# An early 64-byte write into every 256 KB of the output, in an embedding gather with position add

## The chip, the cores and the metric

One core of one Trainium2 chip. The metric is the device time of one execution in microseconds (us), the median of several runs. Times are compared only with those of the kernel before on the same occasion, on the same chip. For what lies inside a trace, traces of different occasions are compared as well.

## The reference

```
indices [32, 512] int32 below 50000; embedding_table [50000, 512] f32; position_embed [512, 512] f32
out[b, s, :] = embedding_table[indices[b, s], :] + position_embed[s, :]        # [32, 512, 512] f32
```

16,384 rows of 2,048 B are gathered from random places of a table of 102.4 MB, and 33.55 MB are written. Nothing is computed but one add per element.

## The kernel before

A sequence's 512 rows lie as 4 rows on each of 128 partitions. GpSimd (POOL) issues 128 gathers of 128 rows, VectorE (DVE) adds the position block in place, and SyncE (SP) stores two gathers at a time (one at a time for the first four and the last four). There are 23 slots of 1 MB, so that no gather waits for a slot before the 24th sequence.

```python
        load_pos(nc.sync, 1)
        # ... (all indices)
        nc.sync.wait_ge(s_pos[half - 1], 16)
        load_pos(nc.sync, half)
        nc.sync.wait_ge(s_gather[0], 16)
        load_pos(nc.sync, half + 1)

        nc.gpsimd.memset(ones[:], 1.0).then_inc(s_ident, 1)
        # ...
        for g, (b, k) in enumerate(order):
            # ... (waits for the index tiles; for a slot from the 24th sequence on)
            ins = nc.gpsimd.indirect_dma_start(
                out=slots[b % SLOTS][:, k, :], out_offset=None, in_=table,
                in_offset=bass.IndirectOffsetOnAxis(ap=where, axis=0),
            ).then_inc(s_gather[g % LANES], 16)
        # ...
            nc.vector.tensor_tensor(
                out=part, in0=part, in1=pos_ps[:, k, :], op=add
            )._wait_ge(s_gather[g % LANES], rounds(g)).then_inc(s_add, 1)
        # ...
        rest = 0
        for adds, b, at, n in stores:
            done = s_out.get(b, s_rest)
            rest += done is s_rest
            nc.sync.dma_start(
                out=out_rows[b][:, at : at + n, :],
                in_=slots[b % SLOTS][:, at : at + n, :],
            )._wait_ge(s_add, adds).then_inc(done, 16)
        nc.sync.wait_ge(s_rest, 16 * rest)
```

## Time and profile before

| | before |
|---|---|
| time, median of 3 runs | 183.71 us (183.7 to 183.91) |
| the execution whose trace is read | 176.13 us, of which the span is 174.4 |
| POOL busy, DVE busy | 121.9 us, 89.0 us |
| DMA | 68.34 MB, 392 GB/s on average |
| last byte of the last store leaves at | 172.50 us of the span |

The traced execution is 7.6 us shorter than the timed ones.

Part 3 and part 6 of the profile page of the kernel before: the DMA queues (packets, MB, share of 16 engines' time), and the issues (count, KB each, median us from issue to landing).

```profile
q1 hardware_dynamic: 11056, 34.76, 49.6%
q0 software_dynamic: 10240, 33.56, 48.9%
...
out_dram<-slot SPq DMA_DIRECT2D x60, 512.0 KB, 6.5
...
slot<-in_embedding_table_dram,idx_t POOLq DMA_INDIRECT x112, 7.3
pos_sb<-in_position_embed_dram SPq DMA_DIRECT2D x4, 256.0 KB, 3.9
...
idx<-in_indices_dram SPq DMA_DIRECT2D x1, 4.0 KB, 1.6
```

Gathers (q0) and plain transfers (q1) share the 16 DMA engines half and half, and together take 98.5% of their time.

### The profile page before, as it was taken

Reading aid. Unit: us, or ns where it says so; the run is one execution under the profiler, and the core shown is the slowest. Engines: PE = TensorE matmul, PEld = TensorE weight load, DVE = VectorE, ACT = ScalarE, POOL = GpSimd, SP = SyncE. Lnnn points to the kernel's source line nnn. Section 1 sums busy time; section 2 is a strip of 40 time slices with the busy share of each in tenths; the row PEclk is TensorE's granted clock in tenths of the full one; section 3 lists DMA queues with packets and bytes.
Section 4 is the critical chain, followed back from the end, with each engine's and each line's share of the span. In section 5 each row is a group of like instructions: output and inputs, shape, how many; then the busy total and the mean of one; then the engine's idle time right before and its main releaser. Section 6 shows DMA issues by size and latency. Waiting matters only on the chain.

```text
span 174.4 us, 427 instructions
## 1 busy us (share of the span) xinstructions
PE 1.0 (1%) x4; PEld 0.4 (0%) x4; DVE 89.0 (51%) x133; ACT 3.6 (2%) x5; POOL 121.9 (70%) x134
## 2 busy tenths in 40 slices
PE   0001100000000000000000000000000000000000
PEld 0000000000000000000000000000000000000000
DVE  0316744745555546455655555555555555555550
ACT  2210000000000000000000000000000000000000
POOL 4777777777777777777777777777777777777200
DMA  3889999999999999999999999999999999999994
GB/s 100 251 260 399 364 385 398 398 396 413 417 418 415 416 420 420 419 420 418 419 420 417 419 421 418 420 419 419 419 418 420 419 419 420 420 417 420 418 413 169
DMA packets 21299, 68.34 MB, mean 392 GB/s; under 512 B 3760, under 2 KB 3888, under 8 KB 21296
## 3 DMA queue, kind: packets, MB, share of 16 engines
q1 hardware_dynamic: 11056, 34.76, 49.6%
q0 software_dynamic: 10240, 33.56, 48.9%
q14 instruction: 3, 0.02, 0.0%
HBM read 34.75 MB, written 33.55 MB: 392 GB/s over the span
## 4 chain that ended last, share of the span: by engine, by line
POOL 65%; issue 22%; DMA 8%; DVE 1%; POOLq 1%; SPq 0%
POOL slot L141 65%; DMA slot<-in_embedding_table_dram,idx_t 4%; DMA slot<-in_embedding_table_dram,idx 3%; DMA idx<-in_indices_dram 1%; DVE idx_t L170 1%; POOLq L149 1%; DVE slot L176 0%; POOLq L136 0%; SPq L221 0%; POOLq L133 0%; SPq L102 0%
## 5 line engine op out<-in xcount | busy, mean ns | idle before, releaser
L141 POOL DMA_INDIRECT slot<-in_embedding_table_dram,idx_t x112 | 105.9, 945 | 34.1 <-issue 34.1
L176 DVE TENSOR_TENSOR slot<-slot,pos_ps 128x512 f32<-128x512 f32 x128 | 87.8, 687 | 80.8 <-DMA slot<-in_embedding_table_dram,idx_t 63.0
L141 POOL DMA_INDIRECT slot<-in_embedding_table_dram,idx x16 | 15.3, 958 | 5.9 <-issue 4.3
L182 ACT COPY pos_ps<-pos_sb 128x512 f32<-128x512 f32 x4 | 2.4, 589 | 8.8 <-DMA pos_sb<-in_position_embed_dram 8.8
L182 ACT ACT_TABLE_LOAD x1 | 1.3, 1283 | 1.0 <-SPq L102 1.0
L170 DVE CAST idx_t<-turned 32x128 int32<-32x128 f32 x4 | 1.1, 280 | 0.1
L154 PE MATMUL turned<-ident,idx_f 128*32 128x128 f32 x4 | 1.0, 416 | 16.9 <-DVE idx_f L164 16.9
L122 POOL MEMSET ones<- 128x128 f32 x1 | 0.2, 204 | 0.5 <-SPq L102 0.5
L154 PEld LDWEIGHTS turned<-ident,idx_f 128*32 128x32 f32 x4 | 0.4, 134 | 17.0 <-DVE idx_f L164 16.9
L123 POOL TENSOR_SCALAR_AFFINE_SELECT ident<-ones 128x128 f32<-128x128 f32 x1 | 0.3, 287 | 0.1
L210 POOL MEMSET const-float32-0.0<- 128x1 f32 x1 | 0.1, 98 | 0.3 <-issue 0.3
L164 DVE CAST idx_f<-idx_raw 128x128 f32<-128x128 int32 x1 | 0.2, 220 | 0.0
L210 POOL MEMSET const-uint8-127<- 128x1 uint8 x1 | 0.1, 115 | 0.0
L210 POOL MEMSET const-bfloat16-1.0<- 128x1 bf16 x1 | 0.1, 109 | 0.0
L210 POOL MEMSET const-float32-1.0<- 128x1 f32 x1 | 0.1, 101 | 0.0
## 6 DMA issues: line engine op xcount, KB each, us to landing
out_dram<-slot SPq DMA_DIRECT2D x60, 512.0 KB, 6.5
out_dram<-slot SPq DMA_DIRECT2D x8, 256.0 KB, 4.8
slot<-in_embedding_table_dram,idx_t POOLq DMA_INDIRECT x112, 7.3
pos_sb<-in_position_embed_dram SPq DMA_DIRECT2D x4, 256.0 KB, 3.9
slot<-in_embedding_table_dram,idx POOLq DMA_INDIRECT x16, 6.0
idx_raw<-in_indices_dram SPq DMA_DIRECT2D x1, 128.0 KB, 3.2
idx<-in_indices_dram SPq DMA_DIRECT2D x1, 4.0 KB, 1.6
idx<-in_indices_dram SPq DMA_DIRECT2D x1, 12.0 KB, 2.6
```

Of the source, the lines that this page charges most:

```text
L122: nc.gpsimd.memset(ones[:], 1.0).then_inc(s_ident, 1)
L123: nc.gpsimd.affine_select(out=ident[:], in_=ones[:], pattern=[[-1, P]], compare_op=mybir.AluOpType.is_equal, fill=0.0, base=0, channel_mul ...
L141: ins = nc.gpsimd.indirect_dma_start(out=slots[b % SLOTS][:, k, :], out_offset=None, in_=table, in_offset=bass.IndirectOffsetOnAxis(ap=whe ...
L149: nc.gpsimd.drain()
L154: ins = nc.tensor.transpose(turned[:, k].rearrange("p b j -> p (b j)"), idx_f[:, :, k], ident[:])
L164: nc.vector.tensor_copy(out=idx_f[:].rearrange("r p k -> r (p k)"), in_=idx_raw[:, :, 0])._wait_ge(s_raw, 16).then_inc(s_cast, 1)
L170: nc.vector.tensor_copy(out=idx_t[j * Q : (j + 1) * Q, :, :], in_=turned[:, :, :, j]).then_inc(s_idx, 1)
L176: nc.vector.tensor_tensor(out=part, in0=part, in1=pos_ps[:, k, :], op=add)._wait_ge(s_gather[g % LANES], rounds(g)).then_inc(s_add, 1)
L182: nc.scalar.copy(out=pos_ps[:, k, :], in_=pos_sb[:, k, :])._wait_ge(s_pos[k], 16).then_inc(s_ps, 1)
L210: nc = _bacc.Bacc("TRN2", target_bir_lowering=False, num_devices=1)
```

## The change

The intent: if the first write to a part of the output is slow, pay for it while the DMA engines have little to do, so that the stores don't. One DMA on the scalar engine's queue, before anything else there, writes 64 B at the start of each of 128 pieces of 256 KB. The stores overwrite these bytes; the sync engine waits for the touch before its first store.

```diff
+    s_touch = sem("s_touch")
...
+        nc.scalar.dma_start(
+            out=out.rearrange("b (c r) d -> (b c) r d", c=P // B)[:, 0, 0:16],
+            in_=ones[:, 0:16],
+        )._wait_ge(s_ident, 1).then_inc(s_touch, 16)
...
+        nc.sync.wait_ge(s_touch, 16)
         rest = 0
         for adds, b, at, n in stores:
```

## The prediction

> **What bounds the kernel now.** I read the page first (engine shares, slices, DMA issues), then the chain that ended last, then the waits, then a table of windows, and last the single DMA packets that the trace records.
>
> The chain of the whole span, and the waits of the engine that starts the gathers:
>
> ```profile
> POOL 65%; issue 22%; DMA 8%; DVE 1%; POOLq 1%; SPq 0%
> ...
> POOL slot L141 <- issue: 38.4, 126, 0.3
> POOL slot L141 <- DMA idx<-in_indices_dram: 1.3, 1, 1.3
> ...
> POOL slot L141 <- DVE idx_t L170: 0.3, 1, 0.3
> ```
>
> The reader is to see that the chain lies on POOL, which writes one gather's descriptors after another (0.95 us busy, 0.30 us to the next), and that POOL hardly ever waits for data: one 1.3 us wait for the first indices, one of 0.3 us at the hand-over to the second index tile. The last gathers are at the same pace:
>
> ```profile
> 160.61 0.94 POOL L141 DMA_INDIRECT slot<-in_embedding_table_dram,idx_t  x1 [0.30 <-issue]
> 161.60 0.69 DVE L176 TENSOR_TENSOR slot<-slot,pos_ps 128x512 f32<-128x512 f32 x1 [0.76 <-DMA slot<-in_embedding_table_dram,idx_t]
> 161.86 0.95 POOL L141 DMA_INDIRECT slot<-in_embedding_table_dram,idx_t  x1 [0.30 <-issue]
> ```
>
> The second gather starts at 4.34 us and the 128th at 161.86: (161.86 - 4.34) / 126 = 1.250 us each. One gather brings 128 x 2,048 B = 262,144 B and its sum is stored once, so this pace asks 524,288 B / 1.25 us = 419 GB/s of the DMA engines. The slices and the windows show that they give just that, and no more:
>
> ```profile
> DMA  3889999999999999999999999999999999999994
> GB/s 100 251 260 399 364 385 398 398 396 413 417 418 415 416 420 420 419 420 418 419 420 417 419 421 418 420 419 419 419 418 420 419 419 420 420 417 420 418 413 169
> ...
> 6.00:8.00 2.00, 0.00 (x0) 0.00 (x0) 0.71 (x2) 0.38 (x1) 1.48 (x2) 1.00 0.82 246
> 8.00:10.00 2.00, 0.00 (x0) 0.00 (x0) 0.67 (x1) 0.00 (x0) 1.61 (x2) 1.00 0.74 154
> 10.00:12.00 2.00, 0.00 (x0) 0.00 (x0) 0.36 (x1) 0.59 (x1) 1.39 (x3) 1.00 0.88 253
> ...
> 60.00:100.00 40.00, 0.00 (x0) 0.00 (x0) 21.99 (x32) 0.00 (x0) 30.25 (x33) 1.00 1.03 419
> ```
>
> In the window lines the last two columns are the busy share of the DMA engines and GB/s. From 60 us on the engines are full at 419 GB/s. From 6 to 12 us they are 74 to 88% busy but move only 154 to 253 GB/s: packets are slow there. Gathers issued into that stretch leave a backlog: the first gather landed 3.8 us after its issue, the typical later one 7.3 us (DMA issues of the page), and the last still 7.32 us. Supply and capacity are equal, so a backlog of about 7.3 - 3.8 = 3.5 us is never worked off, and **the span ends when the DMA engines have emptied it**. Two limits therefore sit within 3.5 us of each other: POOL's pace, and the DMA engines' work plus what they lost early.
>
> So the change is worth what it gives back of DMA time lost before about 60 us, and at most about 3.5 us of 183.71 (1.9%), since below that POOL's pace holds the end.
>
> **What the Trainium skill says.** "DMA: Bandwidth & Descriptors", section Specifications, gives 512 B as the least size at line rate and says that below it the engine does a read-modify-write: the 64 B touches are of that kind; no trace here shows such a write yet. The same page, section "Where 436 GB/s comes from", puts the fabric's ceiling at 435 GB/s; the trace agrees in size, 419 to 421 GB/s being the most a full slice holds. The same page, section "Issuing engines are not separate DMA queues", says that DMAs from the scalar, sync and gpsimd engines end on the same 16 engines and interleave; the trace agrees in that gathers (49%) and plain transfers (50%) share 16 engines' time. Its section "Anatomy of one DMA" puts most of the fixed cost of about 2 us on the receipt from the target memory; the smallest load of the trace (4 KB) took 1.6 us from issue to landing. I found no page that says a first access to a part of HBM is slow, on which the intent of the change rests.
>
> **The change part by part.** It removes nothing. It adds one DMA of 128 rows of 64 B (8,192 B), one row at the start of each of 128 pieces of 256 KB of the output, a wait on it ahead of the first store, and a semaphore.
>
> - *Issue on ScalarE.* It waits for the memset of the ones, which ends at 1.02 + 0.20 = 1.22 us; a DMA issue on the sync engine's sequencer takes 0.33 to 0.49 us, so I expect about 0.4 us, to 1.65. Then the activation table load (1.28 us, at 0.97 before) moves to about 1.7 and ends near 3.0. The first copy waits for the first position block until 4.35. Off the path: 0.
> - *The wait ahead of the stores.* Small loads landed 1.6 to 3.2 us after issue, so the touch should land between 3 and 4.5 us, allowing up to 6 if its packets are slow. The first store goes at 7.47 us, after its add. Slack of 3 us, and the sync engine was blocked on two earlier waits anyway (until 5.79 and about 6.75). Cost: 0.
> - *DMA time.* 8 small packets per engine. Shortest packets in the records take 7 to 9 ns; at ten to twenty times that for a read-modify-write to HBM, 8 x 0.1 to 0.2 = 0.8 to 1.6 us per engine, in 3 to 5 us, where the engines are 66 to 89% busy. The first-gather indices land at 2.61, before it. Delay of the position loads and the first gathers: 0 to 0.5 us, and part of it lies beside idle time. I book +0.1 us.
> - *The gain meant.* If the first write to a piece of the output is slow, the stores' packets should show it. I compared every packet with the usual duration of its size (159 ns for 4,096 B, 84 ns for 2,048 B) and summed the excess over 16 engines. Gathers: 1.27 us before 12 us and 1.51 after, falling off until 60 us and zero after 70. Plain queue after 12 us: 0.03 us, although 33.51 of the 33.55 MB of output leave after 12 us, always into pieces not written before. From 70 us on, 22.1 MB of stores go out without one noticeably slow packet. Before 12 us that queue lost 0.40 us between 7.4 and 12, but there it was still carrying the last position loads: the 512 packets of 2,048 B of those lie ahead of the stores in it, and 488 such packets had started by 11 us. So **the slow stretch comes before the stores' first bytes**, and belongs to the gathers from the random table rows and the position loads, which the touch doesn't reach. Gain: at most some 0.2 us.
>
> Sum: +0.1 (up to +0.5) of added DMA work, -0.1 (up to -0.2) of store packets saved: 183.71 + 0 to 0.1, so 183.8 us.
>
> **The rivals.** *The first write to a region costs, and the touch pays it in idle time.* For it: the first store, issued at 7.47 us, took 6.5 us to land, against 2.9 for the last, and the bad stretch of 6 to 12 us starts around its issue; a slow write could hold up gathers behind it without showing in its own record. Against it: the gathers' slow packets fade with time while untouched output is reached at an even rate to the end. If it holds for the first stores only, some 1 to 2 us of backlog go: 181.7 to 182.7; the ceiling is 180.2.
>
> *The touch itself is slow, and the stores wait for it.* If each of an engine's 8 writes took as long as the slowest gather packets (1.9 us), the touch would need 15 us, the first store would slip from 7.5 to some 17 us, and early gathers would suffer beside it. For it: single packets of 0.4 to 0.8 us already occur at 2.5 to 5 us. Against it: they are a minority, and stores to new pieces are at normal speed. The lost early DMA time, some 1 to 4 us, would go straight to the end: 185 to 188.
>
> *The touch delays the ninth gather.* That gather's add precedes the second index tile, and POOL took it up with 0.3 us or less of slack (20.4 us). A late ninth gather would stall POOL. But the backlog of 3.5 us keeps the DMA engines fed, so a slip of under 3 us changes nothing at the end.
>
> **Range and chances.** Timed runs scatter by 0.2 us. The range takes in a lucky saving of 1.1 us and a loss of 1.4 us: 182.6 to 185.2. Faster by over 2% needs under 180.04, below the ceiling of the gain: 0.03. Slower by over 2% needs over 187.4, the second rival at its worst: 0.03. Within 2%: 0.94.
>
> **What would show it.** Right: POOL still issues every 1.25 us; the touch lands before 6 us; the first store still goes near 7.5 us; the stretch of 6 to 12 us still moves some 150 to 250 GB/s; late gathers still take 7.2 to 7.4 us from issue to landing. Wrong towards faster: that stretch near 400 GB/s and late gathers under 6 us. Wrong towards slower: a wait of the sync engine on the touch, a first store after 8 us, and a lower rate in the first two slices. The weakest step is to read the stores' innocence from their own packet records: if a slow write shows up in other queues' packets, the gain is undercounted.

## The result, and the profile after

| occasion | before | changed | ratio (95% interval) |
|---|---|---|---|
| first | 183.70 us (4 runs) | 183.71 us (4 runs) | 1.0000 (0.9983 to 1.0017) |
| second | 176.73 us (11 runs) | 176.66 us (6 runs) | 0.9997 (0.9959 to 1.0035) |

A ratio is the mean time of one kernel's fast runs over that of the other's of the same rounds, so not quite the ratio of the medians. The change makes no difference on either occasion, though the two differ by 7 us for both kernels. The first row alone proves little: experiments 4 and 8 show that on that kind of occasion the time hardly follows the last byte.

The trace of the first occasion lost most of its semaphore records, so waits and landings can't be read from it. I show the trace of the second, which is complete. First the slices of the changed kernel and its DMA queues, q10 being the touch:

```profile
DMA  3999999999999999999999999999999999999992
GB/s 104 260 319 356 352 374 386 412 413 418 419 417 420 416 418 420 418 420 420 420 419 419 420 420 419 420 418 420 420 418 417 419 418 420 420 420 419 420 402 107
...
q1 hardware_dynamic: 11056, 34.76, 49.3%
q0 software_dynamic: 10240, 33.56, 49.0%
q10 hardware_dynamic: 144, 0.01, 0.1%
```

The engines are full at 416 to 420 GB/s from the tenth slice to the 38th, much as before (413 to 421). Next its issues and landings, and then the windows of the stretch that the prediction says must stay slow (last columns: DMA share, GB/s):

```profile
out_dram<-slot SPq DMA_DIRECT2D x60, 512.0 KB, 6.5
...
slot<-in_embedding_table_dram,idx_t POOLq DMA_INDIRECT x112, 7.1
...
out_dram<-ones ACTq DMA_DIRECT2D x1, 8.0 KB, 1.6
```

Stores take 6.5 us to land, as before, and the touch landed 1.6 us after its issue. The windows:

```profile
6.00:8.00 2.00, 0.00 (x0) 0.00 (x0) 0.69 (x1) 0.12 (x1) 1.52 (x2) 1.00 0.83 240
8.00:10.00 2.00, 0.00 (x0) 0.00 (x0) 0.69 (x1) 0.59 (x1) 1.56 (x2) 1.00 0.83 234
10.00:12.00 2.00, 0.00 (x0) 0.00 (x0) 0.20 (x1) 0.00 (x0) 1.39 (x3) 1.00 0.94 313
...
60.00:100.00 40.00, 0.00 (x0) 0.00 (x0) 22.02 (x32) 0.00 (x0) 30.25 (x33) 1.00 1.03 419
```

The stretch stays: 234 to 313 GB/s at 83 to 94% busy, where before had 154 to 253. A second trace of the kernel before (below) has 193 to 316, so the difference is within the scatter. (The prediction's own sign, 150 to 250 GB/s, was too narrow.) The last gather lands 7.2 us after its issue, as it expected. The same trace's start, in order of time:

```profile
1.25 0.37 ACTq L124 DMA_DIRECT2D out_dram<-ones  x1
...
1.66 1.28 ACT L190 ACT_TABLE_LOAD   x1 [1.66 <-POOL ident L131]
...
4.48 0.59 ACT L190 COPY pos_ps<-pos_sb 128x512 f32<-128x512 f32 x1 [1.53 <-DMA pos_sb<-in_position_embed_dram]
...
7.21 2.36 SPq L200 DMA_DIRECT2D out_dram<-slot  x2
```

The touch is issued at 1.25 us and has landed by 2.8; the first store goes at 7.21 us. The sync engine's wait on the touch costs nothing.

By the packet records, the last byte leaves at 172.63 and 172.90 us in the two traces of the changed kernel, and at 172.50 and 172.57 in the two of before.

### The profile page after: what moved, and what is told of

Read it like the earlier page. It is cut to its first block, busy times and chain, and to the rows that moved or that the text cites. A ratio compares the mean times of both kernels' runs of the same rounds, so it can differ in the third digit from the quotient of the medians.

```text
span 182.5 us, 429 instructions
## 1 busy us (share of the span) xinstructions
PE 1.0 (1%) x4; PEld 0.4 (0%) x4; DVE 89.2 (49%) x133; ACT 3.6 (2%) x5; POOL 122.3 (67%) x134
## 4 chain that ended last, share of the span: by engine, by line
POOL 60%; issue 24%; DMA 5%; DVE 4%; POOLq 0%; SPq 0%
POOL slot L149 60%; DVE slot L184 4%; DMA slot<-in_embedding_table_dram,idx_t 4%; DMA idx<-in_indices_dram 1%; POOLq L157 0%; SPq L230 0%; SPq L103 0%
```

## The experiments

The theories. **A**: the stores' first writes cost nothing that the touch could save; the slow stretch belongs to the gathers and loads. **B**: first writes are slow and hold up everything, gathers included, and the gain is lost somewhere. **C**: the touches are too sparse.

"Excess" below is, as in the prediction, the time of DMA packets beyond the usual one of their size, summed and divided by 16 engines.

**1. Hold the stores back (hold_stores).** The kernel before, with

```diff
+        nc.sync.wait_ge(s_add, 12)
         rest = 0
```

> The kernel before, with the first store held until the 12th add (about 23 us instead of 7.5). Theory A (the slow stretch belongs to the gathers and loads, not to the stores): the gathers' packets lose as much as before between 6 and 12 us (1.27 us per engine before 12 us; I expect over 0.8), though no store is in flight; the rate there stays under 260 GB/s. Rival B (the first writes to the output hold up everything): the gathers' excess before 12 us falls under 0.4 us per engine, and a slow stretch appears where the stores now start, at 23 to 28 us. Time: up to 8 us longer under either, since DMA work is put off.

Measured: 184.55 us against 183.47, ratio 1.0065 (1.0049 to 1.0082). The first store went at 21.50 us. The windows of its trace:

```profile
6.00:8.00 2.00, 0.00 (x0) 0.00 (x0) 0.69 (x1) 0.29 (x1) 1.64 (x2) 1.00 0.82 247
8.00:10.00 2.00, 0.00 (x0) 0.00 (x0) 0.69 (x1) 0.00 (x0) 1.45 (x2) 1.00 0.78 229
...
16.00:20.00 4.00, 0.22 (x2) 0.00 (x0) 3.23 (x8) 0.00 (x0) 3.08 (x4) 1.00 0.71 210
```

From 6 to 10 us the stretch is as slow as ever, with no store in flight. The gathers' excess before 12 us is 0.93 us per engine, above the 0.8 of theory A and far from the 0.4 of B. B falls for these 4 us: writes to the output can't hold up gathers 10 us before there are any. The rate from 10 to 12 us was 349 GB/s, over the 260 that I expected of A. Runs with the stores at their usual time scatter from 229 to 372 GB/s there, so these 2 us decide nothing.

B had a second sign, a slow stretch where the stores now start. Here it is faint: 202 GB/s from 22 to 24 us, 395 in the next 2 us, 318 in the next. It is clear in hold_24 (experiment 8).

**2. Read a small part of the table (narrow_1mb).** The kernel before, with each index tile passed through

```diff
+        nc.vector.tensor_single_scalar(
+            out=idx0_m[:, 0, :], in_=idx0[:, 0, :], scalar=511,
+            op=mybir.AluOpType.bitwise_and,
+        )._wait_ge(s_first, 16).then_inc(s_mask, 1)
```

(three such instructions; the result is wrong).

> The kernel before, with every index cut to its low 9 bits, so that all gathers read the first 1 MB of the table (wrong result on purpose), output pieces untouched as before. Theory A: slow packets of the gathers all but vanish (2.8 us per engine before, under 0.6 here), 6 to 12 us moves well over 300 GB/s, late gathers land in under 6 us, the time falls by 1 to 3.5 us. Rival B: the slow stretch stays, because the output is as untouched as ever; time within 0.5 us of before.

Measured: 183.64 against 183.47 us, ratio 1.0007 (0.9991 to 1.0024). Its windows:

```profile
6.00:8.00 2.00, 0.00 (x0) 0.00 (x0) 0.69 (x1) 0.27 (x1) 1.69 (x2) 1.00 0.81 248
8.00:10.00 2.00, 0.00 (x0) 0.00 (x0) 0.69 (x1) 0.59 (x1) 1.40 (x2) 1.00 0.78 178
10.00:12.00 2.00, 0.00 (x0) 0.00 (x0) 0.10 (x1) 0.00 (x0) 1.44 (x2) 1.00 0.92 308
```

**A miss of mine.** The slow packets stay: 2.61 us per engine, against 2.77 before. So the part of A that put the slow stretch on *random rows all over the table* falls. The output was as untouched as before, so by itself this run can't tell A from B; the run above does, for 6 to 10 us.

**3. Sixteen times the touches (touch_x16, touch_x16_again).** The changed kernel with one touch every 16 KB (shortened here: `in_` is given as what takes effect, and the memset on POOL that fills `ones16`, for which the touch waits, is left out):

```diff
-            out=out.rearrange("b (c r) d -> (b c) r d", c=P // B)[:, 0, 0:16],
-            in_=ones[:, 0:16],
+            out=out.rearrange("b (c q r) d -> (b c) q r d", c=P // B, q=16)[:, :, 0, 0:16],
+            in_=ones16[:],
```

> The changed kernel with a touch of 64 B every 16 KB, 2,048 touches in place of 128. In the changed kernel 144 packets took 0.09 us per engine. Theory A: nothing is gained by denser touching, 16 times the packets take 1.2 to 2 us per engine before 6 us, the first store slips by up to 1.5 us, the time grows by 0 to 1.5 us. Rival C (the touches were too sparse for what a first write costs): the time falls by over 0.5 us.

> Touches every 16 KB once more, for the same reason. Its last byte left at 172.8 us, 0.3 us after that of the first trace of before. Theory A: 0 to 0.6 us longer than before where there is no tail; rival C (sparse touches miss what is slow): shorter by 0.5 us or more.

Measured: ratio 1.0001 (0.9984 to 1.0017) on the first chip, 1.0016 (0.9981 to 1.0050; 177.02 against 176.73 us) on the second. C falls for pieces down to 16 KB: denser touches save nothing. The slow stretch is also there with all these pieces touched (266, 253 and 229 GB/s from 6 to 12 us on the first chip). The last byte leaves at 172.78 and 173.36 us, none earlier than before. The queue of the touches, and their landing, on the second occasion:

```profile
q10 hardware_dynamic: 2064, 0.13, 0.8%
...
out_dram<-ones ACTq DMA_DIRECT2D x1, 128.0 KB, 4.8
```

2,064 packets took 1.42 us per engine, so 1.42 x 16 / 2,064 = 0.011 us each, as do the 144 of the changed kernel (0.09 x 16 / 144 = 0.010 us). Even 16 times the touches end (1.4 + 4.8 = 6.2 us) before the first store, at 8.13 us. They do cost something: POOL waited 0.5 and 0.6 us in the two traces for the second load of indices, at its third gather, where the kernel before doesn't wait.

**4. The end of the timed runs (stores_act).** In the changed kernel's first trace the last byte leaves at 172.63 us but the span is 182.5. I call the time from the last byte to the end of the span the tail. Its slices, beside those of before in the prediction:

```profile
DMA  4789999999999999999999999999999999999700
GB/s 102 236 310 393 345 355 418 410 412 412 419 420 417 418 420 419 418 419 420 419 419 419 418 419 419 419 420 419 418 419 419 419 420 419 418 419 419 278 0 0
```

In the last two slices nothing moves. There the trace shows the sync engine's closing sequence, with five instructions of 0.69 to 1.40 us; in the first trace of before those of that sequence take 0.007 to 0.028 us. To see whose tail it is, the kernel before was run with all stores and the last wait on the scalar engine:

```diff
-            nc.sync.dma_start(
+            nc.scalar.dma_start(
                 out=out_rows[b][:, at : at + n, :],
...
-        nc.sync.wait_ge(s_rest, 16 * rest)
+        nc.scalar.wait_ge(s_rest, 16 * rest)
```

> The kernel before, with all 68 stores and the last wait on the scalar engine; they start after its copies, at about 13 us instead of 7.5. It asks about the end: in the changed kernel's trace the last byte leaves at 172.6 us but the span ends at 182.5, with instructions of the sync engine taking 0.7 us each. Theory D (that tail belongs to the engine that issued the stores as such): it moves to the scalar engine and the time stays within 2 us of before. Theory E (it is peculiar to the sync engine): the tail goes and the time falls by 5 to 8 us. The later stores cost up to 2 us.

Measured: 182.31 against 183.47 us, ratio 0.9935 (0.9919 to 0.9952). Neither theory held: the tail stayed on the sync engine, which now issued no store, but shortened to 178.7 - 172.7 = 6.0 us. The gain is in the tail, for the last byte leaves at 172.68, no earlier. The spans of the timed runs fell by some 3 us (178.7 to 179.4, against 182.2 to 182.3), the time by only 1.2: part of the time lies outside the core's span, and that part grew.

**5. The kernel before once more (before_again), and half of it (half_work).** The second has `for b in range(FIRST, B // 2)` in its order of work (the last sequence's number and the semaphores of the slots are fitted to it), and leaves half of the output unwritten.

> The kernel before, unchanged, for a second trace. The first trace of it ran 174.4 us, ended 1.9 us after the last byte and holds 3,248 semaphore records of transfers; every later trace holds some 410 and ends 6 to 10 us after the last byte, on the sync engine. If that tail belongs to how these runs are recorded and not to the change, this trace has it too: last byte at 172.4 to 172.9 us, span 182.0 to 182.6, sync engine instructions of 0.7 us at the end. If the change brought the tail, it is absent here.

> The kernel before with the first 16 of 32 sequences only (half the output is left unwritten, wrong on purpose). Theory T (the tail grows with the amount of work recorded before it): last byte near 92 us, tail about half, 4 to 6 us. Theory U (a fixed end sequence): tail 9 to 10 us as with all the work. Either way the bad stretch of 6 to 12 us stays.

Measured: before_again 183.64 us, span 182.4, last byte at 172.57, and the tail's instructions at the same places as in the changed kernel's trace. So **the tail isn't the change's doing**. Its windows:

```profile
6.00:8.00 2.00, 0.00 (x0) 0.00 (x0) 0.69 (x1) 0.59 (x1) 1.48 (x2) 1.00 0.78 222
8.00:10.00 2.00, 0.00 (x0) 0.00 (x0) 0.69 (x1) 0.00 (x0) 1.60 (x2) 1.00 0.71 193
10.00:12.00 2.00, 0.00 (x0) 0.00 (x0) 0.69 (x1) 0.48 (x1) 1.39 (x3) 1.00 0.95 316
```

These are the scatter against which a change of the stretch has to be read. half_work took 96.57 us, its last byte at 93.06 us and its span 94.9: no more of a tail than the 1.9 us of the first trace of before, which neither of my two theories expected. The stretch stayed slow, as expected (211 and 207 GB/s from 6 to 10 us).

**6. The third and fourth position loads at once (pos_early).**

```diff
-        nc.sync.wait_ge(s_pos[half - 1], 16)
         load_pos(nc.sync, half)
-        nc.sync.wait_ge(s_gather[0], 16)
         load_pos(nc.sync, half + 1)
```

> The kernel before with the third and fourth position loads issued at once, at 3.4 to 4.3 us, in place of 5.8 and 6.8. Theory A2 (the loads that compete with the gathers make the bad stretch): the rate at 6 to 10 us, with only gathers and the first stores left, no longer has packets over 1 us, the third to sixth gathers land in under 5 us in place of 6.0 to 6.6, the backlog shrinks and the last byte leaves 0.5 to 1.5 us earlier. Theory G (gathers are slow there whatever else runs): third to sixth gathers still 5.5 us or more, last byte within 0.4 us of 172.5. Time within 0.6 us of before in both cases, for the tail takes up the difference.

Measured: 183.63 against 183.59 us, ratio 1.0001 (0.9985 to 1.0018). Its windows:

```profile
8.00:10.00 2.00, 0.00 (x0) 0.00 (x0) 0.69 (x1) 0.82 (x2) 1.61 (x2) 1.00 1.01 399
10.00:12.00 2.00, 0.00 (x0) 0.00 (x0) 1.60 (x3) 0.36 (x1) 1.39 (x3) 1.00 1.08 321
12.00:16.00 4.00, 0.00 (x0) 0.00 (x0) 1.51 (x3) 0.00 (x0) 3.09 (x4) 1.00 0.84 283
```

The stretch moved: 8 to 10 us now carries 399 GB/s, 12 to 16 us only 283 (about 407 before). From a gather's start to its add's, the third to sixth took 5.45, 4.83, 5.02 and 6.20 us, which fits neither theory; the first two rose from 3.9 and 3.7 to 6.0 and 6.1. The last byte left at 172.83 us, as theory G had it. Inconclusive: the loads shift the slow stretch, but don't explain it.

**7. Most stores on the scalar engine (stores_mix).** As in 4, with the first 6 stores on the sync engine: `(nc.sync if adds <= 8 else nc.scalar).dma_start(...)`.

> The kernel before with the first 6 stores on the sync engine and the other 62, with the last wait, on the scalar engine. With all stores there the time fell by 0.65% although the stores began late. If the gain is the shorter tail of a sync engine with little to do, the time is again 182.0 to 182.6; if the late stores cost something, it falls to 181 to 182.

Measured: 182.57 against 183.59 us, ratio 0.9947 (0.9930 to 0.9964). Span 179.4, last byte 173.51. Again what is gained is tail. These two are the only versions that were faster than the kernel before, by 0.5 and 0.65%, and only on chips that have the tail; without it they weren't tried.

**8. Hold the stores longer, and three quarters of the work (hold_24, work_24).** As in 1 with the 24th add, and as half_work with 24 sequences.

> The kernel before with the first store held until the 24th add. Held until the 12th, the last byte left 4.3 us later (176.8 against 172.5) and the time rose only 1.1 us, the tail shrinking from 9.9 to 5.8 us. If the tail ends at a fixed point near 182 us and swallows what comes earlier, then with the last byte near 180 to 182 us the tail is down to 2 to 4 us and the time is 184.5 to 187. If the tail is simply added, the time is 188 to 192.

> The kernel before with the first 24 of 32 sequences (wrong on purpose). With 16 the last byte left at 93.1 us and the span ended 1.8 us later, no tail. If the tail comes with how long the program has run, and only late (above some 165 us), there is none here: last byte near 133 us, span 135. If it grows with the work from the half on, the tail is 3 to 6 us.

Measured: on this chip the kernel before itself took 176.21 us (7 runs), with spans of 174.1 to 175.2, so the tail was absent, and work_24 (136.45 us, span 134.3) says nothing about it. hold_24 took 187.57 us, ratio 1.0642 (1.0602 to 1.0683), and answers another question. The trace is complete; its windows:

```profile
16.00:20.00 4.00, 0.08 (x1) 0.00 (x0) 3.34 (x8) 0.00 (x0) 3.08 (x4) 1.00 0.71 209
20.00:30.00 10.00, 0.00 (x0) 0.00 (x0) 5.51 (x8) 0.00 (x0) 7.56 (x9) 1.00 0.70 209
...
100.00:160.00 60.00, 0.00 (x0) 0.00 (x0) 31.07 (x46) 0.00 (x0) 45.38 (x49) 1.00 1.03 419
```

Until the stores start, at 35.98 us, the engines carry the gathers alone, at POOL's pace of 262,144 B / 1.25 us = 210 GB/s. POOL isn't delayed (last gather at 161.88 us). Yet the last byte leaves at 183.99 us, 11.5 later than in the first trace of before, and the time rises by 0.0642 x 176.21 = 11.3 us. By 60 us the engines had moved 280 GB/s on average, against 358 in that trace of before; the difference, 78 x 60 = 4,680 KB, takes 11.2 us at 419 GB/s. DMA work that is put off is not made up: **the DMA engines' work sets when the last byte leaves**. The backlog shows in the landings: 11.3 us for the later gathers, against 7.3 before. Where there was a tail (hold_stores, beside before_again), the last byte left 176.84 - 172.57 = 4.3 us later, and the time rose by 1.1 us only: the tail shrank from 9.9 to 5.8 us and swallowed most of the rest. On the occasions with the tail, the spans of all full runs with the stores on the sync engine ended at 182.0 to 182.7 us, and still at 182.6 to 183.2 us in hold_stores. **A time taken there says little about shifts of the last byte by a few microseconds.**

The first 6 us after the stores' new start are slow:

```profile
36.00:38.00 2.00, 0.00 (x0) 0.00 (x0) 0.69 (x1) 0.00 (x0) 1.49 (x2) 1.00 0.88 248
38.00:40.00 2.00, 0.00 (x0) 0.00 (x0) 0.69 (x1) 0.00 (x0) 1.60 (x2) 1.00 0.88 261
40.00:42.00 2.00, 0.00 (x0) 0.00 (x0) 0.09 (x1) 0.00 (x0) 1.39 (x3) 1.00 1.00 298
```

Stores and gathers that are already issued wait here, so time is lost. This is B's second sign. It isn't regular: in the first trace of before nearly all output bytes leave after 12 us, and 12 to 16 us carries 407 GB/s. The stores' own packets hardly show it (0.15 us of excess per engine in the whole run). **No run tells whether first writes make it**: that would take held stores with the output touched beforehand.

The same trace corrects how the prediction read slow packets. From 12 to 30 us the gathers' excess is 3.3 us per engine, with no store in flight, though each gather's add starts 3.5 to 4.1 us after the gather's start, much as the first two of before (3.9 and 3.7 us). There the packets take longer while the engines are 70% busy, and nothing is lost by it.

**9. The changed kernel once more (after_again).**

> The changed kernel once more. On one chip the kernel before took 176.2 us and ended 2 us after the last byte; on the others it took 183.5 and ended 10 us after it, in a tail that can hide differences of the last byte. Where the tail is absent, theory A says that the changed kernel is within 0.3 us of before (last byte 172.4 to 172.8 us); a hidden gain of the touch (rival B) would show as 0.5 us or more. If the chip has the tail, only the last byte tells.

Measured: the second row of the result table; its trace is the one shown there. The chip had no tail, and no hidden gain came to light. The interval leaves room for a gain of 0.41%, 0.7 us, at most, and the last byte, at 172.90 us, shows none.

## Why the prediction was right or wrong

The time was right: 183.8 us predicted, 183.71 measured, in the class within 2%. On the first occasion part of that is luck: the tail, which the prediction didn't know of, hid most of hold_stores' loss of 4.3 us, and would probably have hidden a gain too. That the last byte leaves no earlier, and the second occasion, are what bear it out. Step by step:

- **What bounds the kernel.** POOL's pace and full DMA engines are as read; hold_24 shows that DMA work put off comes out in full at the end (11.2 us of work, 11.5 us). But "the span ends when the DMA engines have emptied it" is not so for the timed runs of the first occasion: they end about 10 us after the last byte. The prediction had both numbers, 183.71 timed and 174.4 of span, and let the 9.3 us between them stand unexplained. With a tail that swallows part of a shift (4.3 us became 1.1), its ceiling of 3.5 us was not a ceiling of the metric. No run emptied the backlog, so that ceiling remains untested also for the last byte.
- **Issue on ScalarE.** Right: issue ends at 1.62 us (expected 1.65), the table load starts at 1.66 (1.7), and the first copy still waits for its data, until 4.48.
- **The wait ahead of the stores.** Right, with more slack: landed at 2.8 us (expected 3 to 4.5).
- **DMA time of the touch.** The size was off by a factor of 8 or more: 0.8 to 1.6 us per engine were expected, 0.09 was measured, because each small packet took 0.010 to 0.011 us and not 0.1 to 0.2. The factor of ten to twenty had no measurement behind it. With such packets the second rival had no chance.
- **No gain for the stores.** Right as to the touch, and shown from three sides: the slow stretch is there from 6 to 10 us without a store in flight (hold_stores), touches 16 times as dense save nothing, and the changed kernel is no faster on a chip without a tail. The doubt that the prediction called its weakest step, a slow write showing in other queues' packets, is thereby met for 6 to 10 us. It is not met in general: in hold_24 gathers and stores together are slow for 6 us after the stores' start. A cost of first writes to pieces smaller than 16 KB was not tested either; the stores' packets show at most 0.2 us of excess per engine after 12 us in the traces without touches.
- **Whose the slow stretch is.** "Belongs to the gathers from the random table rows and the position loads" failed in its first half: reading 1 MB of the table in place of 102 MB leaves it (narrow_1mb). For the loads the evidence is mixed (pos_early). What slows the engines there stays open; only the spread of the rows is ruled out, and, from 6 to 10 us, the stores. Nor is packet excess the same as lost time (hold_24), as the sums of 1.27 and 1.51 us took it to be.

What makes the sync engine's closing instructions long is open too. Traces with it hold some 400 to 420 landing records of semaphores, the complete ones of a full run 3,248 or 3,264. But half_work lost records as well (it holds 313) and had no tail, so losing records is not enough. Whether the tail comes from how runs are recorded couldn't be tried.

## What to carry to other kernels

A warm-up is worth doing only if the cold cost is seen in the operations that it would warm: look for slow packets in the stores themselves, and check by moving the stores away from the slow stretch, which takes one added wait. Look at where the stores then start, too: here a slow stretch turned up there, and no run followed it up. A busy DMA engine is not a saturated one; a slow packet is lost time only where other work waits for the engine. And when the timed number and the span of the trace differ by several microseconds, explain that before a gain of one microsecond is argued: here a tail of 10 us, on some chips only, hid most of a shift of 4 us.

## What the Trainium skill lacked or had wrong

- No page tells whether a first write to a part of HBM is slow. No sign of it was found in the stores' own packets here: in the first trace of before, 33.51 MB of stores left after 12 us with 0.03 us of excess per engine, and touching all 2,048 pieces of 16 KB first gained nothing (ratios 1.0001 and 1.0016). The slow 6 us after a late start of the stores (248 to 298 GB/s in hold_24) stay unexplained.
- "DMA: Bandwidth & Descriptors", Specifications, says that below 512 B the engine does a read-modify-write, but gives no time for one. No run here shows the read as such. Packets of the touches' queue took 0.010 to 0.011 us each on average, against 0.084 us for 2,048 B: poor per byte, but negligible for 128 of them.
- The same page, "Anatomy of one DMA", has about 2 us of fixed cost on the gpsimd path only (the prediction set it beside a load on the sync engine's queue, which is not that path); its fit has no counterpart for the scalar engine's queue, where the touch, 8 KB to HBM, landed 1.6 us after its issue in the complete trace.
- I found no page that tells of a sync engine whose closing instructions take about 0.7 us or more each. On the occasions that showed it, the kernel before took 183.5 to 183.7 us, on the others 176.2 to 176.7 us.
